# Attention values of a head pair as one unbroken group of 64-column matmuls

## The chip, the core and the metric

The kernel runs on one core of a Trainium2 chip. A core has a matrix engine (PE), which multiplies a stationary tile of weights with a moving stream of columns, a vector engine (DVE), an activation engine (ACT), a general-purpose engine (POOL) and a queue that issues transfers (SP). The metric is the device time of one execution in microseconds (us). Timed runs give a median; one further execution was recorded by the hardware profiler, and the rows shown below come from that one.

## What is computed

The reference is a two-layer decoder trunk over 256 positions of width 1024. Each layer runs a feed-forward half step, a block of three gated mixers, a cross attention to a memory, and another feed-forward half step. Two of the mixers matter here. Cut to what the change touches:

```
# mixer A, per head (8 heads of 64): three branches, each with a gate
o = gt[0] * (p_cmp @ v_cmp) + gt[1] * (p_sel @ v_sel) + gt[2] * (p_win @ v_win)
# mixer C, per head (8 heads of 64)
o = softmax(q @ k) @ v
x = LN(alpha*x + W_o * sum_b sigmoid(G_b x) * (W_b y_b))
```

## The kernel before

Everything outside the small attention steps is f32 work done as three matmuls on split numbers (`mm3`, L127 to L129: high by high, low by high, high by low); the splits are an ACT copy (L77, tile `wh`) and a DVE subtraction (L78, tile `wl`). The program is written as one sequence of Python calls, and a framework scheduler with its own timeline model decides the order in which each engine executes it; each engine then runs its own list strictly in order and waits at an instruction whose inputs or buffers are not ready.

Inside `mixer`, the attention part is a loop over 12 units: units 0 to 7 are one head each of mixer A (its selected and sliding branches form the two halves of one head's scores), units 8 to 11 are head pairs of mixer C. `unit(u, n)` (L976 to L985 with its loop) does the following:

- It issues `n` fill-in steps (`FILLS`, L34): merge gates (tile `mg`) and branch products (tile `br`), which are plain matmuls that cover the chains of the attention.
- `flip` (L467) turns the weights of the oldest unit: for each of two halves three 128x128 transposes on PE into tile `pt`, and a copy to half of the tile `pT`, the first half by ACT (L474), the second by DVE (L476). There are two `pT` buffers.
- It starts the scores of unit u+2 and their softmax: matmuls into `s`, row minimum on DVE (L453, tile `nm`), four exponentials on ACT (L457), a reciprocal (L459), a product with the gate (L461) and four scalings (L464) on DVE, into tile `p`.
- For mixer A, every second head calls `values_a` (L859), which computes the pair's output in the accumulator `oa`; for mixer C, `values_c` (L942) does the same in `oc`. Both end with an evacuation that splits the sum into two halves (`yhl`).

`values_a` begins with the compressed branch of both heads as one 128-column matmul (L866, stationary tile of two heads of `vc`, moving tile `pc`, which is made at L976 from transposes at L975 in unit 0). Then `weigh` (L480 to L484) is called for each of two branches: per branch, two 64-column matmuls of 256 columns (L482, one per head, each writing its own 64 partitions of `oa`), and two of 128 columns (L484). As nothing ties these together but the accumulator, the scheduler may place each as soon as its own half of `pT` is copied.

The MLA preparation is spread over the units: `mla_norm` after unit 2 (transposes of `cq` and `ckv`, evacuated to `ch`, `cl`, `ckh`, `ckl` at L96 and L97), `mla_q` after unit 3 (36 matmuls into `pq`, in three blocks of 12 by weight block), `mla_kv` after unit 4, and fill-ins follow from unit 4 on. Before unit 8 the query and key of mixer C are transposed (L928 from `qm` and `kf`) and copied by ACT to `qtm` and `ktm` (L929), from which the scores at L935 read.

Of the kernel before, what the change touches and what calls it, by code (L numbers as in the profile page):

```python
# [14 lines left out]
AF = mybir.ActivationFunctionType  # L15
# [3 lines left out]
P = 128  # L19
D = 1024  # L20
S = 256
NT = S // P
# [17 lines left out]
def trunk(ctx, tc, a, out):  # L40
    nc = tc.nc
    V, A, G, T = nc.vector, nc.scalar, nc.gpsimd, nc.tensor
# [14 lines left out]
    def half(shape, dt=F32, name="h"):  # L57
        return m2.tile(shape, dt, tag="m2", name=name)

    def pacc(shape, name="pa"):  # L60
        return acc.tile(shape, F32, tag="acc", name=name)

    def ppw(shape, name="pp"):
        return pw.tile(shape, F32, tag="pw", name=name)

    def small(shape, name):
        n = int(np.prod(shape[1:]))
        if n <= 64:
            return sm.tile(shape, F32, tag=name, name=name, bufs=4 if n <= 16 else 2)
        assert n <= 256  # L70
        return sm.tile(shape, F32, tag="s1", name=name, bufs=4)
# [21 lines left out]
    def evac_hl(h, l, ps, scale=None):  # L93
        if scale is None:
            return split(h, l, ps)
        i = A.activation(h, ps, AF.Copy, scale=scale)  # L96
        return i, V.scalar_tensor_tensor(l, ps, scale, f(h), op0=ALU.mult, op1=ALU.subtract)  # L97

    def wparts(src, n=1024, parts=1):
        raw = wp.tile([P, n], F32, tag="raw", name="raw", bufs=5)  # L100
        h = wp.tile([P, n], F32R, tag="wh", name="wh")
        l = wp.tile([P, n], F32R, tag="wl", name="wl")

        def load(i):
            s = slice(i * n // parts, (i + 1) * n // parts)
            last[0] = nc.sync.dma_start(raw[:, s], src[:, s])
            behind(split(h[:, s], l[:, s], raw[:, s]))

        return (h, l), load

    def wblock(src, n=1024):
        hl, load = wparts(src, n)
        load(0)
        return hl
# [91 lines left out]
    start = [wparts(a["w13"][0, 0, 0, j], parts=4) for j in range(2)]  # L206
# [259 lines left out]

    def flip(p):  # L467
        pT = wk.tile([P, 2, P + S], F32, tag="pT", name="pT", bufs=2)
        for i in range(2):
            pt = ppw([P, P + S], "pt")  # L470
            for b in range(3):
                T.transpose(pt[:, b * P:(b + 1) * P], p[:, i, b * P:(b + 1) * P], ident)
            if i == 0:
                A.activation(pT[:, i, :], pt, AF.Copy)  # L474
            else:
                V.tensor_copy(pT[:, i, :], pt)  # L476
        return pT


    def weigh(pair, start):  # L480
        for o, v, pT in pair:
            T.matmul(o, v[0], pT[:, 0:S], start=start, stop=False, skip_group_check=True)  # L482
        for o, v, pT in pair:
            T.matmul(o[:, P:S], v[1], pT[:, S:S + P], start=False, stop=True, skip_group_check=True)  # L484

    kc_blk = const.tile([P, 2, 32], F32, name="kc_blk")
    V.memset(kc_blk, 0.0)
# [2 lines left out]
    def mixer(l, xT, first, pre):  # L490
# [175 lines left out]
        vs = xp.tile([P, NT, 4, 64], F32, tag="vs", name="vs")  # L666
# [40 lines left out]
        for t in range(NT):  # L707
# [4 lines left out]
            o = 1 - t  # L712
# [98 lines left out]
        vc = half([P, 8, 64], name="vc")  # L811
# [46 lines left out]
        wait = []  # L858

        def values_a(h, pT):  # L860
            wait.append(pT)
            if h % 2 == 0:
                return
            j = h // 2
            oa = pacc([P, S], "oa")
            T.matmul(oa, vc[:, 2 * j:2 * j + 2, :].rearrange("p h d -> p (h d)"), pc, start=True, stop=False,  # L866
                     skip_group_check=True)
            for br in range(2):
                weigh([(oa[i * 64:(i + 1) * 64], [vs[:, t, br * 2 + h // 4, :] for t in range(NT)], wait[i][:, br])
                       for i in range(2)], False)  # L870
            wait.clear()
            evac_hl(yah[:, j, :], yal[:, j, :], oa)


        qm, kf, vm = [], [], []
# [65 lines left out]

        def values_c(u, pT):  # L942
            o = pacc([P, S], "oc")
            weigh([(o[w * 64:(w + 1) * 64], [vm[t][:, 2 * u + w, :] for t in range(NT)], pT[:, w]) for w in range(2)], True)
            evac_hl(ych[:, u, :], ycl[:, u, :], o)


# [19 lines left out]
        pc = small([P, S], "pc")  # L967

        def unit(u, n):
            fill(n)  # L970
            pT = flip(ahead.pop(0))
            if u == 0:
                pt = ppw([P, S], "pt")
                for t in range(NT):
                    T.transpose(pt[:, t * P:(t + 1) * P], scm[:, t].rearrange("p h n -> p (h n)"), ident)  # L975
                V.tensor_copy(pc, pt)  # L976
            if u + 2 < 12:
                ahead.append(soften_a(u + 2) if u + 2 < 8 else soften_c(u + 2 - 8))
            if u < 8:
                values_a(u, pT)  # L980
            else:
                values_c(u - 8, pT)
# [26 lines left out]
        w = [wblock(a["wo_mix"][l, k]) for k in range(2, 8)]  # L1009
# [251 lines left out]
```

## Time and profile before

| | |
|---|---|
| median of 3 runs | 1567.82 us (1567.16 to 1567.83) |
| profiled execution, its own time | 1567.88 us |
| its span in the trace | 1566.1 us |
| granted PE clock over the span, as a share of full speed | 0.998 |
| PE busy | 1547.7 us of the span |
| DVE, ACT, POOL busy | 1119.9, 887.9, 34.4 us |

A timeline row reads: start, length of the group, engine, source line, operation, output and input tiles, shape, count. A bracket at its end gives the idle time before it and what ended that. An f32 matmul is recorded twice, since it makes two passes; consecutive records of one line are joined, and the matmuls are pipelined, so that start-to-start distances give the cost, not the lengths. All quoted stretches are of the first layer; the second layer runs the same program 772.9 us later.

### The profile page before, as it was taken

What the parts mean: (1) busy time and instruction counts of PE and PEld (TensorE: products, weight loads), DVE (VectorE), ACT (ScalarE), POOL (GpSimd) and SP (SyncE); (2) the same over time, 40 slices, a digit from 0 to 9 for tenths busy, and PEclk for the clock granted to TensorE, in tenths of its full rate; (3) what the DMA queues carried; (4) which work ended last, traced back from release to release, by engine and by line L of the source; (5) the groups of instructions that cost most, each with busy time, mean ns of one, the idle gap of its engine ahead of it and who ended that gap; (6) DMA issues with size and microseconds to landing.
All of it is one profiled execution on the core that took longest, in us unless ns stands there. A gap on an engine that the chain in (4) does not pass through costs nothing.

```text
span 1566.1 us, 24970 instructions
## 1 busy us (share of the span) xinstructions
PE 1547.7 (99%) x9472; PEld 1358.0 (87%) x9472; DVE 1119.9 (72%) x2019; ACT 887.9 (57%) x1580; POOL 34.4 (2%) x32
## 2 busy tenths in 40 slices
PE   9999999999999999999999999999999999999997
PEld 8888898898998888888888888988989988888886
DVE  6687669778776777666676666887786777666666
ACT  6566465566664665555555555746575546455553
POOL 0000000100000000000000000000000000000000
PEclk9999999999999999999999999999999999999999
DMA  8667455562555464566635675356524545555552
GB/s 290 216 210 275 147 163 172 171 225 74 175 176 175 137 211 162 189 203 224 219 127 193 202 235 199 131 160 203 190 85 161 166 156 186 178 175 188 189 189 79
DMA packets 81190, 282.09 MB, mean 180 GB/s; under 512 B 9392, under 2 KB 10672, under 8 KB 81072
## 3 DMA queue, kind: packets, MB, share of 16 engines
q1 hardware_dynamic: 81072, 280.52, 54.8%
q8 instruction: 74, 1.21, 0.3%
q14 instruction: 44, 0.36, 0.1%
HBM read 279.44 MB, written 1.05 MB: 179 GB/s over the span
## 4 chain that ended last, share of the span: by engine, by line
PE 96%; ACT 1%; DVE 1%; issue 0%; DMA 0%; POOLq 0%; POOL 0%; SPq 0%; DVEq 0%; ACTq 0%
PE up L151 20%; PE up L150 9%; PE y L127 7%; PE y L128 7%; PE y L129 7%; PE mg L127 3%; PE mg L128 3%; PE mg L129 3%; PE pn L127 3%; PE pn L128 3%; PE pn L129 3%; PE mk L151 2%; PE qx L151 2%; PE br L127 2%; PE br L129 1%; PE br L128 1%
## 5 line engine op out<-in xcount | busy, mean ns | idle before, releaser
L78 DVE TENSOR_TENSOR wl<-raw,wh 128x1024 fp32r<-128x1024 f32 (+3 forms) x490 | 584.6, 1200 | 163.3 <-ACT wh L77 157.2
L77 ACT ACTIVATE wh<-raw 128x1024 fp32r<-128x1024 f32 (+3 forms) x490 | 503.2, 1037 | 204.1 <-PE y L129 55.7
L151 PE MATMUL up<-xT,wh 128*128 128x512 f32 x1344 | 470.2, 396 | 0.0
L150 PE MATMUL up<-xT,wl 128*128 128x256 f32 x1176 | 327.9, 279 | 0.0
L151 PEld LDWEIGHTS up<-xT,wh 128*128 128x128 f32 x1344 | 245.5, 188 | 48.3
L150 PEld LDWEIGHTS up<-xT,wl 128*128 128x128 f32 x1176 | 221.7, 189 | 7.3
L157 ACT ACTIVATE half<-up 128x256 f32<-128x256 f32 x168 | 64.4, 383 | 197.5 <-PE up L151 197.5
L159 DVE TENSOR_TENSOR half<-up,half 128x256 f32<-128x256 f32 x168 | 71.3, 424 | 96.9 <-ACT half L157 96.8
L128 PE MATMUL y<-wl,gh 128*128 128x512 f32 x352 | 136.3, 389 | 0.0
L127 PE MATMUL y<-wh,gh 128*128 128x512 f32 x352 | 135.4, 390 | 0.0
L129 PE MATMUL y<-wh,gl 128*128 128x512 f32 x352 | 131.9, 389 | 0.0
L127 PE MATMUL mg<-xT,wh 128*128 128x256 f32 x384 | 110.0, 286 | 0.0
L128 PE MATMUL mg<-xT,wh 128*128 128x256 f32 x384 | 109.2, 284 | 0.0
L129 PE MATMUL mg<-xT,wl 128*128 128x256 f32 x384 | 108.9, 284 | 0.0
L128 PEld LDWEIGHTS y<-wl,gh 128*128 128x128 f32 x352 | 66.1, 188 | 14.1
L129 PEld LDWEIGHTS y<-wh,gl 128*128 128x128 f32 x352 | 66.1, 188 | 14.0
L127 PEld LDWEIGHTS y<-wh,gh 128*128 128x128 f32 x352 | 66.1, 188 | 10.9
L127 PEld LDWEIGHTS mg<-xT,wh 128*128 128x128 f32 x384 | 73.5, 191 | 1.9 <-issue 1.1
L127 PE MATMUL pn<-wh,xT 128*128 128x512 f32 (+1 forms) x192 | 74.6, 388 | 0.0
L128 PE MATMUL pn<-wl,xT 128*128 128x512 f32 (+1 forms) x192 | 74.3, 387 | 0.0
L129 PE MATMUL pn<-wh,xT 128*128 128x512 f32 (+1 forms) x192 | 74.1, 386 | 0.0
L128 PEld LDWEIGHTS mg<-xT,wh 128*128 128x128 f32 x384 | 73.5, 191 | 0.4 <-issue 0.3
(418 smaller groups left out, 2871.6 us busy)
## 6 DMA issues: line engine op xcount, KB each, us to landing
raw<-in_w_dram SPq DMA_DIRECT2D x260, 512.0 KB, 3.6
raw<-in_winb_dram SPq DMA_DIRECT2D x64, 512.0 KB, 4.2
raw<-in_wina_dram SPq DMA_DIRECT2D x40, 512.0 KB, 3.5
raw<-in_wbr_dram SPq DMA_DIRECT2D x24, 512.0 KB, 4.2
raw<-in_wk_dram SPq DMA_DIRECT2D x16, 512.0 KB, 3.7
raw<-in_cw_dram SPq DMA_DIRECT2D x16, 512.0 KB, 3.5
raw<-in_wv_dram SPq DMA_DIRECT2D x16, 512.0 KB, 4.0
raw<-in_wq_dram SPq DMA_DIRECT2D x16, 512.0 KB, 4.7
```

Source lines behind the costliest of these rows:

```text
L77: i = A.activation(h, src, AF.Copy)
L78: j = V.tensor_tensor(l, src, f(h), op=ALU.subtract)
L127: T.matmul(o, lhs[0], rhs[0], start=start, stop=False)
L128: T.matmul(o, lhs[0], rhs[1], start=False, stop=False)
L129: latest[0] = T.matmul(o, lhs[1], rhs[0], start=False, stop=stop)
L150: T.matmul(o[:, 0, :], w[1][:, s], both[k][:, 0, :], start=False, stop=False)
L151: T.matmul(o, w[0][:, s], both[k], start=k == 0, stop=k == nk - 1)
L157: A.activation(tmp, ps[:, 1, :], AF.Copy)
L159: V.tensor_tensor(dst, ps[:, 0, :], tmp, op=ALU.add)
```

## The change

`flip` now returns the copies beside `pT`. `weigh` takes all sums of a pair at once: for mixer A the compressed branch (now two 64-column matmuls, one per head, in place of the 128-column one) and the two branches; for mixer C one sum. The first matmul of such a group is given a dependency on all copies: four for a pair of mixer A (two heads, two halves), two for a pair of mixer C.

```diff
     def flip(p):
         pT = wk.tile([P, 2, P + S], F32, tag="pT", name="pT", bufs=2)
+        copies = []
...
             if i == 0:
-                A.activation(pT[:, i, :], pt, AF.Copy)
+                copies.append(A.activation(pT[:, i, :], pt, AF.Copy))
             else:
-                V.tensor_copy(pT[:, i, :], pt)
-        return pT
-    def weigh(pair, start):
-        for o, v, pT in pair:
-            T.matmul(o, v[0], pT[:, 0:S], start=start, stop=False, skip_group_check=True)
-        for o, v, pT in pair:
-            T.matmul(o[:, P:S], v[1], pT[:, S:S + P], start=False, stop=True, skip_group_check=True)
+                copies.append(V.tensor_copy(pT[:, i, :], pt))
+        return pT, copies
+    def weigh(sums, copies):
+        first = True
+        for n, pair in enumerate(sums):
+            parts = [(o, v[0], pT[:, 0:S]) for o, v, pT in pair]
+            if len(pair[0][1]) > 1:
+                parts += [(o[:, P:S], v[1], pT[:, S:S + P]) for o, v, pT in pair]
+            for m, (o, v, x) in enumerate(parts):
+                i = T.matmul(o, v, x, start=n == 0 and m < 2, stop=n == len(sums) - 1 and m >= len(parts) - 2,
+                             skip_group_check=True)
+                if first:
+                    for c in copies:
+                        tc.add_manual_dep(i.ins, c.ins.name, mybir.DependencyInfo(
+                            mybir.DependencyClass.Sync, mybir.DependencyReason.DATA), reason="all weights")
+                first = False
...
             oa = pacc([P, S], "oa")
-            T.matmul(oa, vc[:, 2 * j:2 * j + 2, :].rearrange("p h d -> p (h d)"), pc, start=True, stop=False,
-                     skip_group_check=True)
+            out = [oa[i * 64:(i + 1) * 64] for i in range(2)]
+            sums = [[(out[i], [vc[:, 2 * j + i, :]], pc) for i in range(2)]]
             for br in range(2):
-                weigh([(oa[i * 64:(i + 1) * 64], [vs[:, t, br * 2 + h // 4, :] for t in range(NT)], wait[i][:, br])
-                       for i in range(2)], False)
+                sums.append([(out[i], [vs[:, t, br * 2 + h // 4, :] for t in range(NT)], wait[i][0][:, br])
+                             for i in range(2)])
+            weigh(sums, wait[0][1] + wait[1][1])
...
             o = pacc([P, S], "oc")
-            weigh([(o[w * 64:(w + 1) * 64], [vm[t][:, 2 * u + w, :] for t in range(NT)], pT[:, w]) for w in range(2)], True)
+            weigh([[(o[w * 64:(w + 1) * 64], [vm[t][:, 2 * u + w, :] for t in range(NT)], pT[0][:, w]) for w in range(2)]],
+                  pT[1])
```

The scheduler orders the mixer anew under these dependencies. Three places follow, all in the first layer.

On PE, around the second head pair, the program before has the first matmuls of the MLA query (`pq`) between the transposes of `ckv` and of the heads' weights (`pt<-cst,p`); the matmuls are listed as instructions, of which an f32 one is two records in the trace.

```order
L127 MATMUL pq<-wh,ch 128x384 [waits Activation_49]
L128 MATMUL pq<-wl,ch 128x384
L127 MATMUL pq<-wh,ch 128x384
L128 MATMUL pq<-wl,ch 128x384
L127 MATMUL pq<-wh,ch 128x384
L128 MATMUL pq<-wl,ch 128x384
L885 MATMUL pt<-cst,ckv 128x128 [waits DVE_49]
L885 MATMUL pt<-cst,ckv 128x128
L129 MATMUL pq<-wh,cl 128x384 x3
```

In the changed program the same place on PE reads:

```order
L473 MATMUL pt<-cst,p 128x128 [waits DVE_49]
L473 MATMUL pt<-cst,p 128x128 x2
L488 MATMUL oa<-pc,vc 64x256 [waits DVE_49]
L488 MATMUL oa<-pc,vc 64x256
L488 MATMUL oa<-pT,vs 64x256 x2
L488 MATMUL oa<-pT,vs 64x128 x2
L488 MATMUL oa<-pT,vs 64x256 x2
L488 MATMUL oa<-pT,vs 64x128 x2
L127 MATMUL pq<-wh,ch 128x384
L128 MATMUL pq<-wl,ch 128x384
L129 MATMUL pq<-wh,cl 128x384
```

All 36 `pq` matmuls now stand behind the second pair's group, whose first matmul waits for the DVE copy of head 3's transposes; between the transposes of `cq` and that group PE holds only transposes and one head's scores.

On DVE, at the fourth head (head 3, whose row minima are the rows just ahead), the order before is the copy of head 2's transposes, the row minima of head 4 (`s_4097`, `s_4098`), an evacuation (`yhl`), and then head 3's reciprocal.

```order
L476 COPY pT<-pt 128x384 [waits PE_49]
L453 ISA p,nm<-s_4097,cst 128x256 [waits PE_49]
L453 ISA nm 128x1
L453 ISA p,nm<-s_4097,cst 128x256
L453 ISA nm 128x1
L453 ISA p,nm<-s_4098,cst 128x128 [waits PE_49]
L453 ISA nm 128x1
L78 TENSOR_TENSOR yhl<-oa,yhl 128x256 [waits Activation_49]
L453 ISA p,nm<-s_4098,cst 128x128
L453 ISA nm 128x1
L459 RECIPROCAL w<-w 128x4 [waits Activation_49]
```

In the changed program the reciprocal and the scalings of head 3 come first (head 4's scores are `s_4098` and `s_4099` here):

```order
L459 RECIPROCAL w<-w 128x4 [waits Activation_49]
L461 TENSOR_TENSOR w<-w,gt 128x4 [waits DVE_49]
L464 TENSOR_SCALAR p<-p,w 128x256 [waits DVE_49]
L464 TENSOR_SCALAR p<-p,w 128x256
L464 TENSOR_SCALAR p<-p,w 128x128 x2
L477 COPY pT<-pt 128x384 [waits PE_49]
L453 ISA p,nm<-s_4098,cst 128x256 [waits PE_49]
L453 ISA nm 128x1
L78 TENSOR_TENSOR yhl<-oa,yhl 128x256 [waits Activation_49]
```

The copy of head 2's transposes and everything behind it on DVE now wait until head 3's exponentials on ACT are done. (In the second layer the copy of head 2 still comes ahead of that reciprocal; the `pq` matmuls are behind the second group there too.)

On PE, ahead of unit 8, the program before has pieces of the last `oa` group and merge gates behind the transposes of `qm` and `kf`:

```order
L928 MATMUL pt<-cst,qm 96x128 [waits Activation_49]
L928 MATMUL pt<-cst,qm 96x128 x3
L928 MATMUL pt<-cst,kf 96x128 [waits DVE_49]
L928 MATMUL pt<-cst,kf 96x128 x3
L866 MATMUL oa<-pc,vc 128x256
L482 MATMUL oa<-pT,vs 64x256
L127 MATMUL mg<-xT,wh 128x256 [waits Activation_49]
```

In the changed program the scores of the first pair of mixer C follow those transposes at once:

```order
L939 MATMUL pt<-cst,qm 96x128 [waits PE_49]
L939 MATMUL pt<-cst,qm 96x128 x3
L939 MATMUL pt<-cst,kf 96x128 [waits PE_49]
L939 MATMUL pt<-cst,kf 96x128 x3
L946 MATMUL s_4616<-ktm,qtm 128x256 [waits Activation_49]
L946 MATMUL s_4616<-ktm,qtm 128x256
L949 MATMUL s_4617<-ktm,qtm 128x128 [waits DVE_49]
L949 MATMUL s_4617<-ktm,qtm 128x128
```

The scores stand directly behind the copies of `qtm` and `ktm` on ACT, with nothing between them. The other eight of these transposes, with their two copies, stand earlier in the changed program's PE list, ahead of the branch products. POOL's list is the same in both programs; on SP, in each layer, the last load of an output weight block (`wo_mix`) stands behind a load of a normalization bias instead of two rows ahead of it.

## Rows read from the trace of the kernel before

**Rows 1.** The page's first part: busy us (share) and instructions by engine.

```profile
PE 1547.7 (99%) x9472; PEld 1358.0 (87%) x9472; DVE 1119.9 (72%) x2019; ACT 887.9 (57%) x1580; POOL 34.4 (2%) x32
```

**Rows 2.** Timeline of PE, first head pair, layer 0.

```profile
372.45 0.70 PE L866 MATMUL oa<-pc,vc 128*128 128x256 f32 x2 [0.97 <-DVE pc L976]
...
374.37 0.85 PE L472 MATMUL pt<-cst,p 128*128 128x128 f32 x6
```

**Rows 3.** Timeline of PE, a group that runs unbroken in the kernel before.

```profile
408.04 0.65 PE L482 MATMUL oa<-pT,vs 128*64 128x256 f32 x4
...
408.74 0.60 PE L482 MATMUL oa<-pT,vs 128*64 128x256 f32 x4
409.17 0.39 PE L484 MATMUL oa<-pT,vs 128*64 128x128 f32 x4
409.49 0.88 PE L472 MATMUL pt<-cst,p 128*128 128x128 f32 x6
```

**Rows 4.** Windows of tile oa: window, us, busy by engine, clock, DMA share, GB/s.

```profile
369.00:392.00 23.00, 6.02 (x36) 3.03 (x36) 0.84 (x2) 0.76 (x2) 1.00 0.15 47
407.00:410.00 3.00, 2.05 (x18) 1.30 (x18) 0.00 (x0) 0.38 (x1) 1.00 0.90 274
417.00:429.00 12.00, 2.69 (x18) 1.54 (x18) 0.00 (x0) 0.00 (x0) 1.00 0.34 125
```

**Rows 5.** Windows of tile oc, an unbroken group and two broken ones.

```profile
437.00:440.00 3.00, 0.87 (x8) 0.49 (x8) 0.42 (x1) 0.38 (x1) 1.00 0.56 175
466.00:475.00 9.00, 3.02 (x16) 1.33 (x16) 0.63 (x2) 0.77 (x2) 1.00 0.40 121
```

**Rows 6.** Timeline of DVE, heads 2 to 4, layer 0.

```profile
374.67 0.18 DVE L459 RECIPROCAL w<-w 128x4 f32<-128x4 f32 x1 [0.24 <-ACT p L457]
...
375.08 1.01 DVE L464 TENSOR_SCALAR p<-p,w 128x256 f32<-128x256 f32 x4
376.00 0.55 DVE L476 COPY pT<-pt 128x384 f32<-128x384 f32 x1
376.47 0.42 DVE L453 CUSTOM_DVE_ANT_0 p<-s,cst 128x256 f32<-128x256 f32 x1
...
378.98 0.42 DVE L453 CUSTOM_DVE_ANT_0 p<-s,cst 128x256 f32<-128x256 f32 x1
...
380.42 0.17 DVE L459 RECIPROCAL w<-w 128x4 f32<-128x4 f32 x1
...
380.70 0.48 DVE L97 SCALAR_TENSOR_TENSOR cl<-pt,vec,ch 128x256 fp32r<-128x256 f32 x1
381.10 1.00 DVE L464 TENSOR_SCALAR p<-p,w 128x256 f32<-128x256 f32 x4
```

**Rows 7.** Timeline of ACT, first exponentials of heads 2 and 3, layer 0.

```profile
372.77 0.51 ACT L457 ACTIVATE p<-p,nm 128x256 f32<-128x256 f32 x1 [1.85 <-DVE nm L453]
...
376.93 0.51 ACT L457 ACTIVATE p<-p,nm 128x256 f32<-128x256 f32 x1 [1.51 <-DVE nm L453]
```

**Rows 8.** Timeline of PE, MLA query beside the heads' transposes, and the first merge gate.

```profile
382.70 0.33 PE L127 MATMUL pq<-wh,ch 128*128 128x384 f32 x1
...
383.74 0.49 PE L472 MATMUL pt<-cst,p 128*128 128x128 f32 x3
...
391.34 0.28 PE L127 MATMUL mg<-xT,wh 128*128 128x256 f32 x1
```

**Rows 9.** Timeline of PE and ACT ahead of unit 8, layer 0.

```profile
415.95 0.60 PE L928 MATMUL pt<-cst,qm 128*96 128x128 f32 x4
...
416.08 1.06 ACT L77 ACTIVATE wh<-raw 128x1024 fp32r<-128x1024 f32 x1 [1.55 <-issue]
...
417.52 0.59 ACT L929 ACTIVATE ktm<-pt 96x512 f32<-96x512 f32 x1
```

**Rows 10.** Windows of all engines at the end, columns as above.

```profile
1556.00:1562.00 6.00, 0.08 (x1) 0.00 (x0) 4.16 (x9) 1.24 (x2) 1.95 (x2) 0.87 0.23 87
```

## The prediction

> **What bounds the kernel now.** I read the page's first part, then the timeline of PE through the attention part of layer 0, then DVE and ACT in the same stretch. PE is busy 1547.7 of 1566.1 us [rows 1]: the kernel is one long PE list, and outside the attention part nothing in this change can matter. So two things count: how many microseconds of PE work the change removes, and how many idle microseconds it opens where PE's list waits for DVE or ACT. The profiled execution took 1567.88 us, 0.06 above the median of 1567.82; the sum is made against it. A measurement of this kernel can tell about 0.2% (3.1 us) from no change.
>
> **What the groups cost.** The values of a mixer A pair are now issued in pieces: 36 records in layer 0's first stretch (two pairs) are busy 6.02 us, 18 in the second 2.05, 18 in the third 2.69 [rows 4]. The second stretch holds the price of an unbroken one: its sixteen passes over `pT` run from 408.04 to 409.49, 1.45 us, and two pairs of 256-column passes side by side take 409.17 − 408.74 = 0.43 [rows 3]. The changed group has the compressed branch in this same form, so I charge 1.45 + 0.43 = 1.88, with 0.07 for its entry (my choice between nothing and the 0.17 that remain of that stretch's 2.05 when 1.45 and 0.43 are taken off): 1.95 a pair. The upper bound for the compressed part, if its two heads did not overlap, is twice 0.43, +0.43 a pair or +3.4 for eight pairs; the lower bound is 0.43 itself. I take the lower, as the row is of the same shape and type. By PE work alone a layer would then gain 6.02 + 2.05 + 2.69 − 4 × 1.95 = 2.96 us.
>
> For mixer C an unbroken group is busy 0.87, and two broken ones 3.02 [rows 5]: 3.02 − 2 × 0.87 = 1.28, and with two mode changes fewer about 1.4 us a layer.
>
> **What waits instead.** The busy sum of the first stretch is not all on the path. Its pieces at 372.45 to 374.37 [rows 2] run while DVE makes the row minima that the next head needs: the old first piece ends its own idle of 0.97 there, and behind it PE would have had nothing. Under the change the group needs all four copies of a pair, so these 1.9 us turn into idle time at the same place: nothing gained, nothing lost.
>
> The second pair is where I expect the loss. Before, the 36 `pq` matmuls fill PE between the heads' transposes (one stands at 382.70, the next transposes of weights at 383.74 with six matmuls between, which is 0.173 each) [rows 8]; the order of the changed program puts all 36 behind the second pair's group, and that group waits for the DVE copy of head 3's transposes. I follow DVE up to that copy. Head 3's exponentials start on ACT at 376.93; head 2's started at 372.77 and released its reciprocal at 374.67, 1.90 later [rows 6, 7]. So head 3's reciprocal comes at 378.83. It now stands ahead of the copy of head 2's transposes. Behind it on DVE, each from its own row's start to the next one's [rows 6]:
>
> reciprocal and gate 375.08 − 374.67 = 0.41; scalings 376.00 − 375.08 = 0.92; copy 376.47 − 376.00 = 0.47, to 380.63. Head 4's row minima and one evacuation, 380.42 − 378.98 = 1.44, to 382.07. One `cl` 0.40, two small copies 0.2 (an estimate, as they do not have a row here), a second `cl` 0.40, to 383.07; then a wait of about 0.3 for head 4's exponentials, which can start only at the first of its minima (376.93 − 376.47 = 0.46 after 380.63 [rows 6, 7]) and take 1.90, to 383.3 with ACT's other copies between. Reciprocal and gate 0.41, third `cl` 0.40, scalings 0.92: 385.0. Two `ckl` 0.80, and the copy of head 3's transposes 0.56: **386.4**.
>
> From about 379.6 to there PE has transposes and one head's scores, and waits for most of it. Then it runs the group (1.95, to 388.3), the 36 `pq` (36 × 0.173 = 6.23), then half a head's transposes and three changes between kinds of work, together some 0.6 (an estimate: six records of transposes are 0.85 long [rows 2], so three at most 0.43, and an entry above at most 0.17): about 395.2, where the merge gates begin. Before, they began at 391.34 [rows 8]. What has been done by then is not quite the same (head 6's scores are already in both sums), so **+3.8 us** a layer. The copy itself is not later than in the kernel before; what is lost is PE work that stood beside the chain and now stands behind it. Nothing else is late next: the merge gates cover the chains of heads 4 to 7.
>
> In the second layer the copy of head 2 still precedes head 3's reciprocal, but `pq` stands behind the group there too, and the same scalings and copies stand before it; I charge the same.
>
> The fourth pair group: 1.95 in place of 2.69 [rows 4], −0.8. The third is unbroken already: 0.
>
> Ahead of unit 8, the transposes of `qm` and `kf` start at 415.95; ACT first runs a weight split (416.08 to 417.05, when `qtm`'s copy starts) and ends the `ktm` copy at 417.52 + 0.59 = 418.11 [rows 9], 2.16 after the transposes' start. Before, PE had the last pair's first pieces and merge gates there; now the scores follow the eight transposes, which take 0.87, directly. **+1.3** if ACT keeps that split ahead; 0 if it is done sooner, which is the other bound.
>
> POOL's list is unchanged. The one moved transfer on SP is an output weight block that is used after the mixers; buffers come free a few microseconds later, in a stretch whose transfers use 0.15 of the DMA engines [rows 4]; I charge nothing, and if that cover is gone it is one weight split, about 1 us [rows 9].
>
> **The sum.** Per layer +3.8 + 1.3 − 0.8 − 1.4 = +2.9; two layers +5.8. 1567.88 + 5.8 = **1573.7 us**, slower by 0.37%.
>
> **Rivals.**
>
> *PE work counts (faster).* If DVE's chain ends earlier than I think (its `cl`, `ckl` and copies interleave better, or ACT's copies are done sooner), the smaller PE sum shows. Each microsecond before 386.4 at which the second group starts brings one back per layer, so no change is reached at about 383.5. With a start at 382.0 and the wait ahead of unit 8 covered as well, a layer gives 3.8 − 4.4 − 0.8 − 1.4 = −2.8: 1567.88 − 5.6 = 1562.3. The end of it is all of the PE work, 2.96 + 1.4, and the old idle 0.97 [rows 2]: 5.3 a layer, 1557.2. Middle 1560. For it speaks that PE's busy share is 99%, so that work saved is time saved wherever a wait is covered; against it that head 3's reciprocal cannot come before 378.83 whatever the order, and that 4 us of DVE work stand in a row behind it. Chance 0.19.
>
> *The stalls are shorter (same).* The wait ahead of unit 8 is covered (−1.3 a layer), or the chain ends 1.5 to 4 us sooner without that: 1564.7 to 1571.0, middle 1568.5; the first alone lies at the upper edge. Chance 0.17.
>
> *The clock falls (slower still).* In the three stretches of the attention the granted clock is 1.00 [rows 4]. In the 6 us after 1556.00 its mean is 0.87, with a remainder of 0.08 us of matmul [rows 10]: full for 4.4 us and half after, so it fell to the lower of its two levels, 1.2 GHz, once PE had done nothing for some 4 us. Under the change PE is idle or on single transposes from the first copies to 374.3, and again in pieces from 379.6 to 386.4. If the clock goes down in the second of these, every matmul behind it takes twice its time until it rises: 2.5 to 5 us lost a layer if that lasts for as much matmul work, 1578.7 to 1583.7. For it speaks the near 7 us of thin work; against it that the idle comes in pieces, with transposes between. Chance 0.12.
> The Trainium skill, "TensorE: Matmul & The Clock Gate", section "Why this matters for your kernels", advises against idle gaps between bursts of matmuls, since the clock steps back after one. It speaks against a change that opens gaps, as this one does. The end of this trace agrees with it [rows 10]; no row shows it inside the kernel.
>
> *The change does not do what it says* would be a group that is still broken up; in the order of the changed program every group is in one piece, so I give that nothing of its own.
>
> **How the numbers follow.** The main case has 0.52: 1571.0 to 1577.5 (the start of the second group and the wait ahead of unit 8 are each known to about 1 us a layer, and the price of the compressed part may add up to 3.4). The others: 0.17, 0.19 and 0.12. Slower by over 0.2% means above 1570.96: 0.52 + 0.12 = 0.64; within 0.2%: 0.17; faster, below 1564.7: 0.19. The range of 8 in 10 is 1562.3 to 1580.5: it leaves out about two thirds of the faster case below and half of the clock case above, 0.13 + 0.06.
>
> **What would show it.** Right: in the changed profile the second `oa` group of layer 0 starts near 386.4, released by DVE's copy of head 3, with 36 `pq` after it and the first merge gate about 3.8 us later than before; idle of PE over 1 us ahead of the first scores of unit 8; each `oa` group near 1.95 and each `oc` near 0.87; PE's busy sum lower by some 8 us, its idle higher by some 14. Wrong: `oa` groups of over 2.3 (the 64-column compressed matmuls do not overlap), a second group that starts before 383.5, PE's idle up by less than the busy sum falls, or a granted clock under 1 anywhere between 371 and 396.

## The result and the profile after

The changed kernel takes 1575.61 us (median of 6, 1575.49 to 1576.17) against 1567.82 before (1567.16 to 1568.32); the ratio is 1.0051, 95% interval 1.0041 to 1.0061. It is slower by half a per cent: the sign and the place were forecast, the size was 5.8 us forecast and 7.8 measured.

The page's first part of the changed kernel, which answers to [rows 1]:

```profile
PE 1545.0 (98%) x9488; PEld 1357.2 (86%) x9488; DVE 1119.8 (71%) x2019; ACT 886.4 (56%) x1580; POOL 36.1 (2%) x32
```

PE's busy sum fell by 2.7 us while the span grew by 7.7, from 1566.1 to 1573.8. So 10.4 us more of the span are idle on PE. The list of PE's waits names four that the kernel before has hardly or not (columns: engine and tile, what was waited for, us in total, times, longest):

```profile
PE pt L473 <- DVE p L464: 6.4, 4, 2.9
PE s L946 <- ACT ktm L940: 2.2, 2, 1.1
PE pt L896 <- DVE nm L453: 2.1, 2, 1.5
...
PE pt L473 <- DVE cl L97: 1.2, 2, 0.9
```

They are 11.9 us. The kernel before has 0.6 of the first, and 1.9 for `pc`, which is gone here, so these waits make 9.4 of the 10.4.

PE's timeline of the changed kernel, layer 0, the stretch of [rows 2] and [rows 8] (start, us, line, tiles, idle before):

```profile
370.64 0.28 PE L864 MATMUL s<-kl,qs 128*128 128x256 f32 x1
373.81 1.08 PE L473 MATMUL pt<-cst,p 128*128 128x128 f32 x6 [2.90 <-DVE p L464]
374.54 0.78 PE L862 MATMUL s<-kh,qs 128*128 128x512 f32 x1
...
376.74 1.11 PE L488 MATMUL oa<-pc,vc 128*64 128x256 f32 x4
377.65 1.50 PE L488 MATMUL oa<-pT,vs 128*64 128x256 f32 x16
379.08 0.55 PE L473 MATMUL pt<-cst,p 128*128 128x128 f32 x3
...
384.10 0.55 PE L473 MATMUL pt<-cst,p 128*128 128x128 f32 x3 [0.88 <-DVE cl L97]
384.68 0.80 PE L862 MATMUL s<-kh,qs 128*128 128x512 f32 x1
...
386.90 1.12 PE L488 MATMUL oa<-pc,vc 128*64 128x256 f32 x4
387.81 1.54 PE L488 MATMUL oa<-pT,vs 128*64 128x256 f32 x16
389.28 0.45 PE L127 MATMUL pq<-wh,ch 128*128 128x384 f32 x1
...
396.71 0.36 PE L127 MATMUL mg<-xT,wh 128*128 128x256 f32 x1
```

The idle time in which the kernel before ran pieces of `oa` is now one hole of 2.90 us. The second group starts at 386.90, all 36 `pq` matmuls follow it, and the merge gates begin at 396.71 instead of 391.34 [rows 8]. One thing in these rows was not in the sum: a score matmul of 512 columns takes 0.78 and 0.80 where it takes 0.48 at the full clock. The windows of 1 us say why (window, length, busy by engine PE, PEld, DVE, ACT, POOL, granted clock, DMA share, GB/s):

```profile
374.00:375.00 1.00, 1.00 (x7) 1.00 (x6) 0.83 (x4) 0.56 (x2) 0.00 (x0) 0.65 0.00 0
375.00:376.00 1.00, 1.00 (x5) 0.81 (x5) 1.00 (x5) 0.00 (x0) 0.00 (x0) 0.50 0.00 0
...
378.00:379.00 1.00, 1.00 (x16) 0.68 (x12) 0.67 (x4) 0.23 (x2) 0.00 (x0) 1.00 0.00 0
...
386.00:387.00 1.00, 1.00 (x7) 0.67 (x8) 1.00 (x6) 0.42 (x2) 0.00 (x0) 0.50 0.00 0
...
388.00:389.00 1.00, 1.00 (x16) 0.70 (x14) 0.46 (x3) 0.44 (x3) 0.00 (x0) 1.00 0.00 0
```

The clock went to its lower level of 1.2 GHz twice in layer 0, after the hole and after the patchy stretch ahead of the second group, and once in layer 1, after the hole (0.50 from 1153 to 1155). The third and fourth group of mixer A and the last two of mixer C, windows of tile `oa` (as [rows 4]) and then of tile `oc` (as [rows 5]):

```profile
412.00:417.00 5.00, 1.95 (x20) 1.28 (x20) 0.41 (x1) 0.38 (x1) 1.00 0.69 210
426.00:430.00 4.00, 1.95 (x20) 1.28 (x20) 0.00 (x0) 0.36 (x1) 1.00 0.19 76
```

```profile
472.00:477.00 5.00, 1.74 (x16) 0.98 (x16) 0.61 (x2) 0.77 (x2) 1.00 0.46 138
```

At the full clock whole groups cost what was forecast: 1.95 for mixer A, 0.87 each for mixer C. The 64-column compressed matmuls do run side by side. The first two groups of layer 0, which begin at the lower clock, take 2.34 (376.74 to 379.08) and 2.38 (386.90 to 389.28).

Where the time went is best read from the same matmul in two timelines. I took the start of head 2's last score (371.20 in layer 0 of the kernel before, 1144.14 in layer 1), and that of the first `y` matmul behind the mixer (485.15 and 1258.13). The shift of the second less the shift of the first is what a kernel costs in that layer; between these places nothing shifts by more than 0.02 us, except in the two kernels that move a merge gate, which are not in the table. "Falls" are the stretches of the clock at 0.5 in that layer. The shifts and falls are those of the one profiled execution of each kernel, the medians those of all.

| kernel | layer 0, us (falls) | layer 1, us (falls) | median, us |
|---|---|---|---|
| the change | +4.49 (2) | +3.87 (1) | 1575.61 |
| 20 extra matmuls in the hole | +2.65 (0) | +3.57 (1) | 1573.60 |
| 20 and 7 extra matmuls | +4.11 (1) | +3.05 (0) | 1575.15 |
| early MLA query | +0.66 (1) | −0.53 (0) | 1568.95 |
| before, MLA query held back | +2.22 (0) | +2.19 (0) | 1572.41 |
| form only | +2.04 (0) | +1.99 (0) | 1571.94 |
| late pairs and mixer C only | −0.75 (0) | −0.79 (0) | 1566.17 |
| mixer C only | −1.44 (0) | −1.49 (0) | 1564.99 |
| first pair without waits | −1.73 (0) | −1.75 (0) | 1564.38 |
| waits only | −1.91 (0) | −1.93 (0) | 1564.16 |
| accumulator opened early | −2.04 (0) | −2.07 (0) | 1563.49 |

In the change's own trace the first layer begins 0.56 earlier than before, since the first matmuls of the program ran at the full clock from 5.65 us on, where the kernel before had it from 10.83 (its matmul at 10.83 stands at 10.16 here); that differs from execution to execution (−0.62 to +0.23 over these kernels) and is no part of the change. 4.49 + 3.87 − 0.56 = 7.8. PE, DVE and ACT run both layers in one order in all of these kernels but the change, the two with extra matmuls and the early query; in those four some instructions of the mixer change places between the layers. Layer by layer the change and the run with 20 extra matmuls have one order, but for one copy on DVE and one evacuation on ACT in layer 0.

### The profile page after: what moved, and what is told of

Read it like the earlier page. It is cut to its first block, busy times and chain, and to the rows that moved or that the text cites. A ratio compares the mean times of both kernels' runs of the same rounds, so it can differ in the third digit from the quotient of the medians.

```text
span 1573.8 us, 25003 instructions
## 1 busy us (share of the span) xinstructions
PE 1545.0 (98%) x9488; PEld 1357.2 (86%) x9488; DVE 1119.8 (71%) x2019; ACT 886.4 (56%) x1580; POOL 36.1 (2%) x32
## 4 chain that ended last, share of the span: by engine, by line
PE 95%; ACT 2%; DVE 1%; issue 0%; DMA 0%; SPq 0%; POOLq 0%; POOL 0%; DVEq 0%; ACTq 0%
PE up L151 20%; PE up L150 9%; PE y L127 7%; PE y L128 7%; PE y L129 7%; PE mg L127 3%; PE mg L128 3%; PE mg L129 3%; PE pn L127 3%; PE pn L129 3%; PE pn L128 3%; PE mk L151 2%; PE qx L151 2%; PE br L127 2%; PE br L128 1%; PE br L129 1%
```

## The experiments

**The same waits, but the accumulator opened early.** The wait for all copies sits on the first matmul that reads `pT`.

```diff
-                if first:
+                if first and (n > 0 or len(sums) == 1):
...
-                first = False
+                    first = False
```

> The change, but the wait for all copies sits on the first matmul that reads pT; the two 64-column compressed matmuls of a pair wait for nothing and may go early, which opens the pair's accumulator. In the order of this kernel 27 of the 36 pq matmuls then stand ahead of the second group again. Theory (the loss is pq standing behind the second group, the wait ahead of unit 8, and the clock that falls in the thin stretches): the second stretch's 3 us and unit 8's 1.1 us a layer come back, 1567 to 1569. Rival (the wait for four copies costs this wherever pq stands): 1574 to 1576. Rival (only the lower clock costs): the idle ahead of the first group remains, so 1573 or more.

Measured: 1563.49, ratio 0.9973 (0.9961 to 0.9984): faster than both kernels, by 4.2 and 12.1 us. Its PE timeline, layer 0:

```profile
383.09 0.77 PE L129 MATMUL pq<-wh,cl 128*128 128x384 f32 x3
...
386.73 1.52 PE L488 MATMUL oa<-pT,vs 128*64 128x256 f32 x16
...
390.03 0.28 PE L127 MATMUL mg<-xT,wh 128*128 128x256 f32 x1
```

The matmuls that wait for all copies start at 386.73, hardly earlier than the group of the change (386.90); but the compressed part and 27 `pq` matmuls have run by then, and the merge gates begin at 390.03. So waiting for all copies is not by itself what costs. It came out below the range expected, probably since I had taken the stretch's cost off the change's total and forgotten that the falls of the clock would go too.

**Waits only**, with the compressed branch as the old 128-column matmul ahead of the group.

```diff
-            sums = [[(out[i], [vc[:, 2 * j + i, :]], pc) for i in range(2)]]
+            T.matmul(oa, vc[:, 2 * j:2 * j + 2, :].rearrange("p h d -> p (h d)"), pc, start=True, stop=False,
+                     skip_group_check=True)
+            sums = []
...
-            weigh(sums, wait[0][1] + wait[1][1])
+            weigh(sums, wait[0][1] + wait[1][1], False)
```

> One part alone: the waits of the change, but the compressed branch stays one 128-column matmul that waits for nothing. pq is ahead of the second group as in the kernel before. Theory: like the run with the early 64-column pair, 1567 to 1569, within 1 us of it, as the form of the compressed matmul is worth 0.1 us a pair or less. Rival (the 64-column form is what costs): this one is 3 us or more faster than the other.

Measured: 1564.16, ratio 0.9978 (0.9969 to 0.9987): below the range expected too, and 0.7 us from the run above, 0.1 us a layer in the traces. The form of the compressed matmul is worth next to nothing where it stands.

**Mixer C only, and the late pairs only.**

```diff
 # mixer C only: values_a as before the change
-            weigh(sums, wait[0][1] + wait[1][1])
...
+                weigh([[(oa[i * 64:(i + 1) * 64], [vs[:, t, br * 2 + h // 4, :] for t in range(NT)], wait[i][0][:, br])
+                        for i in range(2)]], [], False, br == 1)
 # late pairs only: no waits for pairs 0 and 1
-            weigh(sums, wait[0][1] + wait[1][1])
+            weigh(sums, wait[0][1] + wait[1][1] if j > 1 else [])
```

> One part alone: mixer C's groups with the waits, mixer A as before. Theory: the two broken groups of a layer become whole, 1.3 to 1.5 us a layer, nothing else moves: 1564.8 to 1565.3. Rival (the broken pieces lay beside a wait, so nothing is gained): 1567.8.

> The waits for mixer A's third and fourth pair and for mixer C, none for the first two pairs. Theory: mixer C's gain of 1.5 us a layer and the fourth pair's 0.8 us, less a wait of 1.1 to 1.4 us for the copies of qtm and ktm ahead of unit 8: 1565 to 1566.5. Rival (the waits cost at every pair): 1570 or more.

Measured: 1564.99, ratio 0.9982 (0.9973 to 0.9992), and 1566.17, ratio 0.9989 (0.9980 to 0.9998). Mixer C's whole groups bring 1.47 us a layer. The third and fourth pair with their waits take 0.70 of it back: the scores of unit 8 wait for `ktm` there as in the change (2.3 us in two waits), and that wait is longer than what the whole group saves. The other form of the first two pairs has no part in it, as nothing shifts up to head 7's last score in either kernel.

**The MLA query emitted first.** Only the place of `mla_q` moves; all waits stay.

```diff
+            if u == 3:
+                mla_q()
             if u < 8:
                 values_a(u, pT)
...
-            if u == 3:
-                mla_q()
```

> The change, with the MLA query emitted ahead of the second pair's values instead of behind them, so that pq takes its accumulators first; 36 pq matmuls stand ahead of the second group. Nothing else is taken back: the idle of 2.9 us ahead of head 1's transposes and the wait ahead of unit 8 remain. Theory: the second stretch's 3 us a layer come back, and with them the second fall of the clock in layer 0: 1568 to 1570. Rival (the waits themselves cost, pq's place does not matter): 1574 to 1576.

Measured: 1568.95 (1567.68 to 1571.12), ratio 1.0009 (1.0000 to 1.0018). Against the layer of the change without a fall (2.65, below), the layer without a fall here is at −0.53: the query's place is worth 3.2 us a layer (in layer 1 of both it is 0.53 and the 2.55 worked out below, 3.1). The ten executions line up by their mean granted clock: 0.997 in the four at 1567.68 to 1568.42, 0.996 and 0.995 in the next four up to 1570.65, 0.994 in the two at 1570.86 and 1571.12. It is one program, and its time moves by 3.4 us. Only the first execution was traced, with one fall in the mixer, so that the others have more falls is inferred from their mean clock. Three falls take the mean of the change from 0.998 to 0.995, some 0.001 each, so 0.997 to 0.994 would be about three falls.

**The same cost by itself.** The kernel before, with one order edge:

```diff
             if u == 3:
-                mla_q()
+                with tc.issue_after(final[0]):
+                    mla_q()
```

> The disputed cost by itself: the kernel before, with no wait and the old forms, and one order edge that holds all 36 pq matmuls behind the second pair's last value matmul. Theory (pq's place is the main loss): against the clean layers of the runs so far, that place is worth 3.2 us a layer (2.65 us in layer 0 of the run with the filled idle time, where no clock fell, against a gain of 0.53 us in layer 1 of the run with the early query): 1567.7 + 6.4 = 1574, and up to 1576.5 if the clock falls in the thin second stretch. Rival (pq's place costs nothing without the waits): 1567 to 1569.

Here `final[0]` is the second pair's last matmul. Measured: 1572.41, ratio 1.0031 (1.0019 to 1.0043). Without any wait on copies and with no fall of the clock, `pq` behind the second pair costs 2.2 us a layer:

```profile
382.58 0.94 PE L472 MATMUL pt<-cst,p 128*128 128x128 f32 x6 [1.04 <-DVE cl L97]
...
386.30 0.38 PE L486 MATMUL oa<-pT,vs 128*64 128x128 f32 x2
386.62 0.44 PE L127 MATMUL pq<-wh,ch 128*128 128x384 f32 x1
```

Most of the pair's pieces run ahead of the last transposes here, and `pq` starts at 386.62. In layer 0 of the next run, which has the change's whole group and no fall of the clock, it starts at 388.01. Of these 1.39 us that layer begins 0.14 later. The rest, 1.25, is the group's own wait and the first pair's 0.24 (below), and so the missing 1.0 of 3.2. The expectation of 1574 took the whole 3.2 for it and was 1.6 too high.

**The hole filled with extra matmuls.** They write an accumulator that the group then overwrites; `mark[2]` is head 2's last score matmul.

```diff
+            for m, n in (((2, 20),), (), (), ())[j]:
+                with tc.issue_after(mark[m]):
+                    for _ in range(n):
+                        T.matmul(oa, kh[:, 0, 0:P], kh[:, 0, :], start=True, stop=True)
```

> The change, with 20 extra 256-column matmuls into the first pair's accumulator (overwritten by the group's first matmul) in the idle time behind head 2's scores; PE's order is otherwise that of the change. They take 20 x 0.12 = 2.4 us of 2.9 us idle and hold the clock there. Theory: the first fall of the clock goes in both layers; it made the first group 0.5 us (layer 0) and 1.1 us (layer 1) longer and the transposes and scores ahead of it some 0.7 us, of which part is hidden behind DVE: 1573 to 1574.5. Rival (the lower clock costs nothing since DVE's chain sets the time there): 1575.6. Rival (the clock is nearly the whole loss): 1570 or less.

Measured: 1573.60, ratio 1.0037 (1.0024 to 1.0050). PE of this kernel, layer 0:

```profile
371.32 2.56 PE L882 MATMUL oa<-kh 128*128 128x256 f32 x20
374.38 0.84 PE L473 MATMUL pt<-cst,p 128*128 128x128 f32 x6 [0.50 <-DVE p L464]
...
378.50 0.55 PE L473 MATMUL pt<-cst,p 128*128 128x128 f32 x3
...
386.13 0.65 PE L488 MATMUL oa<-pc,vc 128*64 128x256 f32 x4
...
388.01 0.44 PE L127 MATMUL pq<-wh,ch 128*128 128x384 f32 x1
...
395.45 0.36 PE L127 MATMUL mg<-xT,wh 128*128 128x256 f32 x1
```

And windows of its second thin stretch, layer 0 and then layer 1 (the clock is the third number from the end):

```profile
384.00:388.00 4.00, 3.96 (x30) 2.44 (x30) 3.17 (x15) 2.05 (x9) 0.00 (x0) 1.00 0.02 4
...
1160.00:1164.00 4.00, 4.00 (x23) 2.83 (x23) 2.84 (x15) 1.93 (x9) 0.00 (x0) 0.61 0.00 0
```

With 20 useless matmuls more a layer the kernel is 2 us faster. The intervals of the two ratios overlap; the executions do not (1573.31 to 1574.08 against 1575.49 to 1576.17), and the kernel before, timed beside each, moved by 0.14. Layer 0 has no fall and costs 2.65 us: this is the change without the clock, up to the copy and the evacuation named above. Layer 1 lost the fall after the hole and got one after the patchy stretch, which its counterpart in the changed kernel does not have.

**Seven more**, ahead of head 3's second transposes.

```diff
+            if warm is not None and i == 1:
+                for _ in range(7):
+                    T.matmul(pt[:, 0:S], warm[:, 0, 0:P], warm[:, 0, :], start=True, stop=True)
```

> The run with 20 extra matmuls in the first idle time, and 7 more into the tile of head 3's second transposes (overwritten by them), in the idle time of 0.9 us ahead of these; PE's order otherwise that of the change. Theory: no fall of the clock is left in either layer, each layer costs the 2.65 us of layer 0 in the run before, 1567.7 + 5.3 = 1573.0, 0.5 to 1 us under the run with 20 alone. Rival (the fall in layer 1 came by chance of the moment, not of the gap): as the other run, 1573.6, or both falls in either layer.

Measured: 1575.15 (1573.48 to 1576.37), ratio 1.0047 (1.0032 to 1.0062); a miss. Layer 0 has a fall from 383 to 386 with the same order up to there as the run above, in which there was none; layer 1 has none. The rival stands: where the stretch is this thin, whether the clock falls is not set by the program alone. Layer 1 costs 3.05, 0.4 more than the layer without a fall above. Half of that stands where the seven are: from head 3's first transposes to the group it is 3.28 us, against 3.08 in layer 1 of the change, whose clock is at 1.00 there. The other half is not explained.

**A merge gate in the hole**, in the change and in the early-query kernel.

```diff
-FILLS = (7, 0, 0, 0, 1, 2, 2, 2, 4, 4, 4, 0)
+FILLS = (6, 1, 0, 0, 1, 2, 2, 2, 4, 4, 4, 0)
...
-            fill(n)
+            with tc.issue_after(mark[2]) if u == 1 else nullcontext():
+                fill(n)
```

> The change, with one of the merge gates (24 matmuls, 2.9 us) taken from ahead of head 0's transposes and placed in the idle time behind head 2's scores. Theory: 2.9 us a layer come back and the first fall of the clock goes with them, some 3.5 us a layer: 1567 to 1570. Rival (the idle there is not on the path, as DVE's chain behind it sets when the second group starts): 1573 to 1575, since only what PE does behind the second group counts.

> Both: the MLA query ahead of the second group, and a merge gate in the idle time ahead of the first. Theory: the two gains add, 3 us and 3 to 4 us a layer, and mixer C's and the fourth pair's gains remain: 1561 to 1564, faster than the kernel before. Rival (they overlap, as both fill the same wait for DVE): as the better of the two alone, 1567 or more.

Measured: 1575.59 (1574.36 to 1577.97), ratio 1.0047 (1.0030 to 1.0063), and 1568.37, ratio 1.0007 (0.9997 to 1.0016). No gain in either. The first is 0.6 us above the rival's range, the second within it, but not for the rivals' reason. PE of the first of the two, layer 0 (the traced execution is its slowest, 1577.97):

```profile
369.06 1.51 PE L473 MATMUL pt<-cst,p 128*128 128x128 f32 x6 [3.17 <-DVE p L464]
...
372.07 0.41 PE L127 MATMUL mg<-xT,wh 128*128 128x256 f32 x1
...
375.02 0.28 PE L127 MATMUL mg<-xT,wh 128*128 128x256 f32 x1
```

The gate had been covering head 0's softmax. Taken from there it leaves 3.17 us idle ahead of head 0's transposes, and half of it then runs at the lower clock (0.41 us a matmul against 0.28). In layer 0 of the second the same 3.17 us are idle, and the clock stays at 1.00.

**The form only**, 64-column compressed branch, no waits.

```diff
-            weigh(sums, wait[0][1] + wait[1][1])
+            weigh(sums, [])
...
-                  pT[1])
+                  [])
```

> One part alone: the 64-column form of the compressed branch and one accumulation group per pair, no waits. Theory: the form is worth 0.1 us a pair or less and the order of the first two pairs stays that of the kernel before: 1566.5 to 1568.5. Rival (the form itself brings the gain of the runs that open the accumulator early): 1564 to 1565.

Measured: 1571.94, ratio 1.0027 (1.0017 to 1.0037), which neither theory had. Up to unit 6 nothing moved: the shift is −0.62 at head 2's last score and −0.71 at the last branch product before unit 8. The 2 us a layer arise behind it. Without waits the order came out with mixer C's groups in two pieces, three of four in this layer where the kernel before has two, with merge gates or transposes between. One of them on PE:

```profile
437.28 0.65 PE L488 MATMUL oc<-pT,vm 128*64 128x256 f32 x2
...
440.28 0.86 PE L488 MATMUL oc<-pT,vm 128*64 128x256 f32 x6
```

One more broken group is worth some 0.7 of the 2 us, as two made whole brought 1.47; where the rest comes from was not tested.

**The best run, and no wait for the first pair.**

```diff
-            weigh(sums, wait[0][1] + wait[1][1])
+            weigh(sums, wait[0][1] + wait[1][1] if j else [])
```

> The run with the early 64-column pair, and no wait for the first pair, so that its first pieces run in the idle time ahead of head 1's transposes as in the kernel before. Theory: of the 0.84 us idle there about half comes back, less one more change between kinds of matmul a layer: 1562.5 to 1563.7. Rival (DVE's chain sets the time there): 1563.5 to 1565, no better than the run it is taken from.

Measured: 1564.38, ratio 0.9979 (0.9970 to 0.9989); no gain. DVE sets the time there, as the rival had it: head 1's transposes start 3.17 us behind head 2's last score whatever PE does between, in this kernel (370.99 to 374.16), in the change (370.64 to 373.81) and in the kernel before (371.20 to 374.37). Which of this kernel, the waits alone and the early accumulator is fastest, the intervals do not settle.

## Why the prediction was right, and by how much not

**The prices of the groups** held: 1.95 for a pair and 0.87 for mixer C, which came to 1.47 us a layer where 1.4 was forecast.

**The main term** was "All 36 behind the second group, +3.8 a layer". The mechanism is shown from both sides: the early query takes 3.2 us a layer back, and the late query alone costs 2.2. In the layer with the hole filled, at the full clock, the group starts at 386.13, `pq` at 388.01 and the merge gates at 395.45, where 386.4, 388.3 and 395.2 were forecast. But 0.78 us of that stretch are head 6's scores. The sum took them to be done by then in both kernels, while the kernel before runs them behind its first merge gates:

```profile
394.21 0.40 PE L852 MATMUL s<-kh,qs 128*128 128x512 f32 x1
```

So the place of `pq` with the group's wait is 395.45 − 391.34 − 0.78 = 3.3 within one layer, near the 3.2 and below the 3.8. (Nor are all 36 `pq` between the transposes before the change: 27 are, and the last nine stand behind the pair there too.) The chain on DVE was followed closely enough. On DVE of the changed kernel, the row that answers to the copy in [rows 6]:

```profile
384.87 0.87 DVE L97 SCALAR_TENSOR_TENSOR ckl<-pt,vec,ckh 128x256 fp32r<-128x256 f32 x2
385.66 0.55 DVE L477 COPY pT<-pt 128x384 f32<-128x384 f32 x1
```

The copy ends at 386.21, or 386.77 with the earlier start of 0.56 taken out; the forecast was 386.4. That it would be no later than before the change was right too, since there it ends at 386.74:

```profile
386.18 0.56 DVE L476 COPY pT<-pt 128x384 f32<-128x384 f32 x1 [1.14 <-PE pt L472]
```

It is not the group's last releaser, though: PE was still on its own scores and transposes, at the lower clock, until 386.90.

**The first pair**, forecast at nothing gained and nothing lost: 0.24 us a layer, worked out as the early query's −0.53 less mixer C's −1.47 and the late pairs' +0.70. It is a remainder, in which the second pair's whole group is included. The hole itself costs nothing, as forecast: the 3.17 us ahead of head 1's transposes are the same before and after.

**The wait ahead of unit 8**, forecast at +1.3, less 0.8 for the fourth pair: the wait is 1.12.

```profile
421.99 0.60 PE L939 MATMUL pt<-cst,kf 128*96 128x128 f32 x4
423.71 1.13 PE L946 MATMUL s<-ktm,qtm 96*128 96x256 f32 x4 [1.12 <-ACT ktm L940]
```

The net of pairs three and four is +0.70 where +0.5 was forecast. Without the clock layer 0 costs 2.65, where +2.9 was forecast. The terms 3.2, 0.24, 0.70 and −1.47 add up to that by construction, as the first two are differences from it. That the total came so near is partly luck: the main term was 0.6 smaller than forecast, the first pair and the late pairs 0.4 dearer.

**What failed** is the step that put the clock among the rivals as the other case, at 0.12 and 2.5 to 5 us a layer, instead of into the sum. It fell three times in the traced execution of the change, beside the main mechanism and not in its place; all six timed executions have a mean clock of 0.994 or 0.995, against 0.998 before. What a fall costs can be read stretch by stretch against the run with the filled hole, and best in layer 1, where both have the same order and each has one fall, the change after the hole and the other behind the first group (start of the transposes behind the hole, of those behind the first group, and of `pq`; first the change, then the other):

```profile
1151.23 0.84 PE L473 MATMUL pt<-cst,p 128*128 128x128 f32 x6 [2.90 <-DVE p L464]
...
1156.67 0.55 PE L473 MATMUL pt<-cst,p 128*128 128x128 f32 x3
...
1166.14 0.44 PE L127 MATMUL pq<-wh,ch 128*128 128x384 f32 x1
```

```profile
1149.97 0.85 PE L473 MATMUL pt<-cst,p 128*128 128x128 f32 x6 [0.50 <-DVE p L464]
...
1154.09 0.55 PE L473 MATMUL pt<-cst,p 128*128 128x128 f32 x3
...
1164.58 0.44 PE L127 MATMUL pq<-wh,ch 128*128 128x384 f32 x1
```

The first stretch is 5.44 with the fall and 4.12 without, the second 10.49 with it and 9.47 without: 1.32 and 1.02 us. In layer 0, where the change has both falls, the same stretches are 5.27 against 4.12 and 10.20 against 9.51, so 1.15 and 0.69. Layers of one kernel that differ by one fall are 0.92 to 1.19 apart. So a fall costs about 1 us. Without its falls layer 1 of the change costs 3.87 − 1.32 = 2.55 and layer 0 4.49 − 1.15 − 0.69 = 2.65, and some 3.2 us of the 7.8 are the clock's.

The price in the prediction was too high, since it had the lower clock act on work that sets the time. In the second fall the scores take 0.80 for 0.50 us, yet the group starts only 0.2 later, counted from the transposes behind the first group (7.82 against 7.63), as DVE's chain stands beside them; the other 0.5 are the group itself. Two signs that the prediction named against itself were there, a clock under 1 between 371 and 396 and `oa` groups of over 2.3; the second came from the clock and not from matmuls that do not overlap. The idle on PE rose by 10.4 us where 14 were forecast, and its busy sum fell by 2.7 where 8 were, which fits falls that make busy time out of idle: with the accumulator opened early, and no fall in the mixer, the busy sum fell by 7.7 (to 1540.0).

The Trainium skill, "TensorE: Matmul & The Clock Gate", section "Why this matters for your kernels", advises against idle gaps between bursts of matmuls because the clock steps back. The change agrees, with the hole of 2.90 us followed by a clock of 0.5 in both layers; the early query agrees in part, as the same hole of 2.90 us stands in both its layers and the clock fell in layer 0 alone.

**Why `pq` went behind.** The chip runs show what that place costs; why the scheduler chose it is read from the orders alone. `pq` needs four accumulators of a pool of four. In every kernel where something without a wait opens the second pair's accumulator (the old compressed matmul, the new ones without the wait), or where `pq` is emitted first, the order has `pq` between the transposes. In every kernel where the group's first matmul waits for the copies, and nothing else opens it, `pq` stands behind the group. (The late query of the experiments is put behind by its edge.) That the pool hands out its accumulators in the order of the program would explain this, and it fits that 27 `pq` matmuls, nine for each of three accumulators, run ahead while the pair's own is open. It was not tried by itself, for example with a pool of five, so this cause stays open.

## What to carry to other kernels

A wait on the first instruction of a group can hold more than the group: here it put behind the group work that takes its buffers from the same pool, and by the orders, though not by a test, the buffer is the reason. Put such a wait on the first instruction that needs the data and let an instruction without it open the group: here that turned +7.8 us into −4.2. Before filler work is moved into a hole, look at what it covers where it stands; and where a change leaves the matrix engine thin for some microseconds, put a price on the clock beside the idle time, and a spread, as executions of one program differ in it.

## What the hardware showed that was not expected

One program, the early query, ran between 1567.68 and 1571.12 us, in step with its mean clock (0.997 to 0.994). One order of instructions with the hole filled had a fall of the clock in layer 0 in one run and none in the other up to the same place. Twenty matmuls whose result is thrown away made a kernel 2.0 us faster (1575.61 to 1573.60). And the 64-column form of the compressed matmuls costs nothing and gains nothing: in a group that is whole either way, the pair of heads is 1.88 us in one form and 1.98 in the other from the group's first matmul to the one behind it (third pair, form only and mixer C only), and the entry into it takes 0.21 against 0.12.
